# State space stage of a two-block network: a memory tile for each part of a table, two loads into idle buffers, the last inputs scaled behind the first units, and outputs split one step later

## The chip, the cores and the metric

The kernel runs on one core of one Trainium2 chip. The metric is the device time of one execution in microseconds (us), as the median of several runs. A core has five engines that run side by side and meet at semaphores: TensorE (PE, matrix products; its weight loads are listed as PEld), VectorE (DVE), ScalarE (ACT), GpSimd (POOL) and SyncE (SP). Each works through its own instructions in order. SP and ACT also start DMA transfers here, so a transfer that has to wait for a buffer holds up what stands behind it on that engine.

## What is computed

Two blocks on 512 tokens of width 1024 in float32. The first block has two layers; its second layer (index 1) holds the state space mixer that the change is about. Cut to what matters:

```python
h = rms_norm(x, norm_mix[1])
# s5_mixer(h): 64 groups of 16 channels, 64 complex states each
mag = jnp.exp(lr * dt)
ab_re, ab_im = mag * jnp.cos(li * dt), mag * jnp.sin(li * dt)
...
bu_re = jnp.einsum('gpc,bsgc->bsgp', bb_re, uf)
bu_im = jnp.einsum('gpc,bsgc->bsgp', bb_im, uf)
_, _, xr, xi = lax.associative_scan(_complex_affine_combine, (a_r, a_i, bu_re, bu_im), axis=1)
y = (jnp.einsum('gcp,bsgp->bsgc', c_re, xr) - jnp.einsum('gcp,bsgp->bsgc', c_im, xi)
     + d.reshape(S5_GROUPS, S5_GROUP_CH) * uf)
# behind it
g_a, g_b = jnp.split(jax.nn.gelu(y) @ od_w_glu, 2, axis=-1)
x = x + g_a * jax.nn.sigmoid(g_b)
```

Ahead of it lie the first layer's mixer, its convolutional feed-forward network (`conv_ffn`) and a gated side input (`ple`); behind it the second layer's feed-forward network and side input, and the whole second block.

## The kernel before

All activations lie in SBUF with channels on the 128 partitions and the 512 tokens along the free axis, as eight tiles x[0] to x[7]. A matrix product splits each operand into a rounded high part and a low rest (`split`: a cast on ACT, line 308, then a subtraction on DVE, line 311) and adds three products (`mm_fm`, lines 373 to 375). Weights come through SP into `raw` tiles, are cast to `whi` on ACT (line 345) and subtracted to `wlo` on DVE or POOL (line 350).

**Tables.** The mixer works on sequences of four tokens at a time. While `conv_ffn(0)` runs, `s5_tables` makes coefficient tables in sixteen rounds of two quarter tiles and writes them to DRAM (line 1150, on ACT's queue): G (256 columns, makes the scans' input from u), E (256 columns, the rotation's cosine and sine) and C (416 columns, makes the output from u, xr and xi). `CUT` names the columns; `tabs[k]` holds unit k's tables.

**Units.** A unit is one of the eight tiles of 128 channels. `ready(m)` runs as `ple` finishes x[m]: it adds the squares of x[m] to the sum for the norm (`Rms.add`, lines 217 to 225), and `turn_in` scales x[m], writes it to DRAM and reads it back in another order as `up` (four DMAs on SP, line 1247). For m = 1, 3 and 5 it also starts table loads, and for m = 7 it runs a square root on a tile of one column, `warm` (line 1324). When all eight are in, `chain` and `phases` make `rbt`, the factor 1/rms in the order of `up` (lines 174 to 182 and 1339 to 1346; line 177 is the square root on ACT).

A unit then goes through these steps:

- `norm`: up times rbt (line 1250; unit 0 on DVE, the others on POOL)
- `feed`: 16 products on PE, G with up, into two PSUM banks pv (line 1256), and a copy `rm` of the decay (ACT, line 1259)
- `spin`: six DVE instructions that rotate pv by E (lines 1265 to 1270)
- `scan`: two scans along the tokens on DVE (line 1277), giving zr and zi, and products with E that rotate back into xr and xi (lines 1283 to 1295): on POOL for units 0 to 6, on DVE for unit 7; of odd units the difference that gives xr is made by DVE (`real`, line 1295)
- `emit`: products on PE, C with up, xr and xi (line 1303), a gelu on ACT (line 1305), a write to DRAM (line 1306) and a read in the order of the tokens into `y` (four DMAs on SP, line 1310)
- `land`: the split of y into G.h[k] and G.l[k] (lines 308 and 311), the operands of the product with `od_w_glu`.

**Order.** A loop over t runs the units as a pipeline, one step apart: in step t it calls feed(t+1), a load of G for t+3, spin(t), on even t real(t-1), a load of E for t+1 (from t = 2), emit(t-2), a load of C for t, scan(t), land(t-3), and the products of output t-4 with the first weights (`acc0[1]`). At t = 8 the second accumulator `acc0[0]` starts. Table tiles have two buffers for G and C and three for E, y has two. The seven norms of units 1 to 7 stand ahead of the loop. Within these calls the framework's scheduler sets the order on each engine when it builds the program, by order in the code and by when it expects an operand to be ready.

Of the kernel before, what the change touches and what calls it, by code (L numbers as in the profile page):

```python
# [18 lines left out]
P = 128  # L19
# [30 lines left out]
def tile_net(ctx: ExitStack, tc: tile.TileContext, a, out):  # L50
# [5 lines left out]
    def nm(s):  # L56
        uid[0] += 1
        return f"{s}_{uid[0]}"
# [151 lines left out]
    class Rms:  # L210
# [4 lines left out]
        def add(self, m):  # L215
            if self.n == 0:
                act.activation(self.acc, x[m], AF.Square)
            else:
                if self.two and self.n % 2:
                    sq = xp.tile([P, T], F32, tag="diag", name=nm("sq"), bufs=2)  # L220
                else:
                    sq = stile("st_q")
                act.activation(sq, x[m], AF.Square)  # L223
                eng = pool if self.n < 6 else vec
                eng.tensor_tensor(self.acc, self.acc, sq, op=ALU.add)  # L225
            self.n += 1
# [664 lines left out]
    def ple(l, X, rms, done, fins=()):  # L891
        with tc.tile_pool(name=nm("ple"), bufs=1) as pp:
# [73 lines left out]
    r4 = const.tile([P, 32], F32, name="r4")  # L966
    CUT = {"tG": (0, 256), "tE": (704, 960), "tC": (288, 704)}
    tabs = [{z: dr.tile([P, 4, hi - lo], F32, tag=f"{z}{k}", name=f"{z}{k}") for z, (lo, hi) in CUT.items()}
            for k in range(KD)]
    hdr = [dr.tile([P, 4, P], F32, tag=f"hd{k}", name=f"hd{k}") for k in range(KD)]  # L970
# [241 lines left out]
    with tc.tile_pool(name="s5e", bufs=1) as ep, ExitStack() as late:  # L1212
# [6 lines left out]
        class Unit:  # L1219
# [3 lines left out]

            def table(self, tag, bufs):
                lo, hi = CUT[tag]
                t = ep.tile([P, 4, hi - lo], F32, tag=tag, name=nm(tag), bufs=bufs)
                nc.scalar.dma_start(t, tabs[self.k][tag])
                return t

            def load_g(self):  # L1230
                self.G = self.table("tG", 2)

            def load_e(self):
                self.E = self.table("tE", 3)

            def load_c(self):
                self.C = self.table("tC", 2)

# [13 lines left out]
            def feed(self):  # L1252
                self.pv = [bank((P, 4, P)) for _ in range(2)]
                for z in range(2):
                    for i in range(4):
                        pe.matmul(self.pv[z][:, i, :], self.G[:, i, P * z:P * z + P], self.up[:, i, :],
                                  start=True, stop=True)
                self.rm = rms4[self.par]
                act.copy(self.rm[:, :, 1:], r4[:, 4 * self.k:4 * self.k + 4].unsqueeze(2).to_broadcast([P, 4, P - 1]))

            def spin(self):
                pv = self.pv
                er, ei = self.E[:, :, 0:P], self.E[:, :, P:]
                t0, t1 = [xt_(f"X{'hl'[self.par]}{j}") for j in range(2)]
# [7 lines left out]
            def scan(self):  # L1272
# [6 lines left out]
                eng = vec if k == KD - 1 else pool  # L1279
                er, ei = self.E[:, :, 0:P], self.E[:, :, P:]  # L1280
                self.xr, self.xi = xrs[self.par]
# [9 lines left out]
                eng.tensor_tensor(v[1], ei, self.zr, op=ALU.mult)  # L1291
                eng.tensor_tensor(self.xi[:, :, 1:], v[0], v[1], op=ALU.add)

# [3 lines left out]
            def emit(self):  # L1297
                k = self.k
                py = bank((P, 4, P))
                for i in range(4):  # L1300
                    for st, (c, rhs) in enumerate(((288, self.up[:, i, :]), (0, self.xr[:, i, 0:P]),
                                                   (160, self.xi[:, i, 0:P]))):
                        pe.matmul(py[:, i, :], self.C[:, i, c:c + P], rhs, start=st == 0, stop=st == 2)
                g = ep.tile([P, 4, P], F32, tag="h", name=nm("g"), bufs=2)
                act.activation(g, py, AF.Gelu_apprx_tanh)
                nc.scalar.dma_start(hdr[k], g)
                self.y = rp.tile([P, 4, P], F32, tag="y", name=nm("y"), bufs=2)
                src = hdr[k].rearrange("(r c) i n -> i c r n", c=32)
# [11 lines left out]
        def ready(m):  # L1320
            rms2.add(m)
            if m == KD - 1:
                warm = sm.tile([P, 1], F32, tag="warm", name="warm")
                act.activation(warm, eps_r, AF.Sqrt)
            units[m].turn_in()
# [41 lines left out]
        units[0].feed()  # L1367
        units[2].load_g()
        for k in range(1, KD):
            units[k].norm(pool)  # L1370
# [3 lines left out]
        for t in range(KD + 4):  # L1374
# [8 lines left out]
            if t == 2:  # L1383
                acc0[1] = [bank() for _ in range(2)]
            if t > 1 and at(t + 1):
                at(t + 1).load_e()
            if t == KD:
                acc0[0] = [bank() for _ in range(2)]
                mm_fm(acc0[1], w0s[1], G, [4], start=False, stop=False, js=[4])
                for k in range(3):  # L1390
# [5 lines left out]
            if at(t):  # L1396
                at(t).scan()
            if at(t - 3):
                at(t - 3).land()
            if at(t - 4):  # L1400
                k = t - 4
                if t != KD:
                    mm_fm(acc0[1], w0s[1], G, [k], start=k == 0, stop=k == KD - 1, js=[k])
                if t == KD + 1:
# [13 lines left out]
        for c in range(4):  # L1418
# [5 lines left out]
            for j in range(2):  # L1424
                m = 2 * c + j
                sg = rp.tile([P, T], F32, tag="y", name=nm("sg"), bufs=2)
                act.activation(sg, acc0[1][j], AF.Sigmoid)
# [508 lines left out]
```

## Time and profile before

| | us |
|---|---|
| runs: median (lowest to highest of 3) | 2743.25 (2742.7 to 2746.15) |
| the profiled execution | 2745.55 |
| its span, first to last instruction | 2743.8 |
| PE busy | 2692.1 |
| DVE busy | 1562.4 |
| ACT busy | 999.5 |
| POOL busy | 684.0 |

The profile is one execution, seen by the hardware profiler. The span is what the instructions take from first to last; the execution's own time is a little longer. An engine's busy time counts its computing instructions only; waits, branches and the starting of DMAs are not in it. A row of the timeline gives the start in us from the span's beginning, the duration, the engine, the line in the kernel, the operation, what is written and read, the count of instructions merged into the row, and in brackets how long the engine was idle before and what ended that. Names stand without their numbers, so `s` is one of several scratch tiles and `ps` any PSUM bank.

### The profile page before, as it was taken

The page shows a single profiled execution, that of the slowest core. Times are in us where ns is not written, and L with a number is a line of the kernel's source. Part 1 is how long each engine was busy: PE and PEld are TensorE (multiplying, and loading weights), DVE is VectorE, ACT ScalarE, POOL GpSimd, SP SyncE. Part 2 cuts the span into 40 slices and gives each one's busy share as a digit, 9 for nine tenths or more (in the row PEclk, how much of TensorE's full clock was granted, in tenths as well). Part 3 has the DMA queues.
Part 4 walks back from the last instruction along what each step waited for, and adds up shares of the span by engine and source line. Part 5 has one row for each costly group of instructions (what it writes and reads, how often), then busy time and mean ns, then how long its engine had stood idle before and what let it go on. Part 6 is the DMA issues. An engine that isn't in the chain of part 4 may idle for free. (4 is left out here: it accounts for less than half of the span.)

```text
span 2743.8 us, 35312 instructions
## 1 busy us (share of the span) xinstructions
PE 2692.1 (98%) x14355; PEld 2270.6 (83%) x14355; DVE 1562.4 (57%) x2475; ACT 999.5 (36%) x1302; POOL 684.0 (25%) x721
## 2 busy tenths in 40 slices
PE   8999999999799999999999999999999999999998
PEld 8978887887678888888888888888888888888888
DVE  5455989475774746475333335866387755633335
ACT  5543424345433424244212235333343353422222
POOL 2214035553541000002000036454554321200000
PEclk9999999999999999999999999999999999999999
DMA  5214334335652222223322222232322223222231
GB/s 165 73 36 108 100 120 162 122 117 198 223 185 90 96 95 92 93 92 123 107 93 92 92 93 91 89 102 79 98 83 83 92 93 108 78 92 92 93 102 68
DMA packets 278995, 288.79 MB, mean 105 GB/s; under 512 B 20325, under 2 KB 267079, under 8 KB 278832
## 3 DMA queue, kind: packets, MB, share of 16 engines
q1 hardware_dynamic: 243152, 244.65, 27.3%
q10 hardware_dynamic: 34848, 41.46, 4.5%
q8 instruction: 113, 1.85, 0.3%
q0 software_dynamic: 832, 0.41, 0.1%
q14 instruction: 50, 0.41, 0.0%
HBM read 262.90 MB, written 23.59 MB: 104 GB/s over the span
## 5 line engine op out<-in xcount | busy, mean ns | idle before, releaser
L345 ACT CAST whi<-raw 128x2048 fp32r<-128x2048 f32 (+2 forms) x216 | 406.5, 1882 | 777.9 <-PE ps L374 589.5
L373 PE MATMUL ps<-Xh,whi 128*128 128x512 f32 (+1 forms) x1472 | 568.9, 388 | 1.0 <-ACT Xh L308 1.0
L374 PE MATMUL ps<-Xl,whi 128*128 128x512 f32 (+1 forms) x1472 | 564.7, 384 | 1.5 <-DVE Xl L311 1.0
L375 PE MATMUL ps<-Xh,wlo 128*128 128x512 f32 (+1 forms) x1472 | 564.1, 384 | 0.0
L350 DVE TENSOR_TENSOR wlo<-raw,whi 128x2048 fp32r<-128x2048 f32 (+2 forms) x167 | 380.4, 2278 | 318.0 <-ACT whi L345 316.5
L350 POOL TENSOR_TENSOR wlo<-raw,whi 128x512 fp32r<-128x512 f32 (+1 forms) x196 | 248.4, 1299 | 664.8 <-ACT whi L345 340.1
L373 PEld LDWEIGHTS ps<-Xh,whi 128*128 128x128 f32 x1472 | 277.5, 189 | 60.0 <-issue 3.0
L374 PEld LDWEIGHTS ps<-Xl,whi 128*128 128x128 f32 x1472 | 278.7, 189 | 58.2 <-DVE Xl L311 1.4
L375 PEld LDWEIGHTS ps<-Xh,wlo 128*128 128x128 f32 x1472 | 278.1, 189 | 57.0 <-DVE wlo L350 0.4
L373 PE MATMUL ps<-XBh,whi 128*128 128x512 f32 (+1 forms) x736 | 281.9, 385 | 1.0 <-ACT whi L345 1.0
L374 PE MATMUL ps<-XBl,whi 128*128 128x512 f32 (+1 forms) x736 | 281.1, 383 | 0.6 <-POOL XBl L311 0.6
L375 PE MATMUL ps<-XBh,wlo 128*128 128x512 f32 (+1 forms) x736 | 281.6, 384 | 0.0
L375 PE MATMUL ps<-Ah,wlo 128*128 128x512 f32 (+1 forms) x528 | 202.5, 384 | 0.0
L373 PE MATMUL ps<-Ah,whi 128*128 128x512 f32 (+1 forms) x528 | 202.5, 386 | 0.0
L374 PE MATMUL ps<-Al,whi 128*128 128x512 f32 (+1 forms) x528 | 202.1, 383 | 0.3 <-DVE Al L311 0.3
L1604 DVE SCALAR_TENSOR_TENSOR ps<-glu,par,ps 128x512 f32<-128x512 f32 x232 | 170.4, 752 | 3.9
L374 PEld LDWEIGHTS ps<-XBl,whi 128*128 128x128 f32 x736 | 138.2, 188 | 30.6 <-POOL XBl L311 1.0
L375 PEld LDWEIGHTS ps<-XBh,wlo 128*128 128x128 f32 x736 | 138.2, 188 | 29.9
L373 PEld LDWEIGHTS ps<-XBh,whi 128*128 128x128 f32 x736 | 137.7, 188 | 29.5 <-ACT whi L345 1.4
L225 POOL TENSOR_TENSOR st_a<-st_a,st_q 128x512 f32<-128x512 f32 x22 | 38.4, 1747 | 455.1 <-ACT st_q L223 455.0
L382 PE MATMUL ps<-whi,Xh 128*128 128x256 f32 (+1 forms) x512 | 147.4, 289 | 0.5 <-ACT z L616 0.4
L383 PE MATMUL ps<-wlo,Xh 128*128 128x256 f32 (+1 forms) x512 | 144.7, 283 | 0.0
(498 smaller groups left out, 4790.0 us busy)
## 6 DMA issues: line engine op xcount, KB each, us to landing
raw<-in_ffn_w_up_dram SPq DMA_DIRECT2D x66, 1024.0 KB, 5.1
raw<-in_w_in_dram SPq DMA_DIRECT2D x40, 1024.0 KB, 5.1
raw<-in_ffn_w_down_dram SPq DMA_DIRECT2D x32, 1024.0 KB, 4.8
raw<-in_ffn_w_gate_dram SPq DMA_DIRECT2D x22, 1024.0 KB, 5.2
raw<-in_ffn_w_down_dram SPq DMA_DIRECT2D x16, 768.0 KB, 4.2
raw<-in_ev_w_in_dram SPq DMA_DIRECT2D x8, 1024.0 KB, 5.2
raw<-in_ple_w_gate_dram SPq DMA_DIRECT2D x8, 1024.0 KB, 5.1
raw<-in_od_w_glu_dram SPq DMA_DIRECT2D x8, 1024.0 KB, 5.8
```

What stands on the lines that cost most here:

```text
L225: eng.tensor_tensor(self.acc, self.acc, sq, op=ALU.add)
L345: cp = act.copy(hi, rv)
L350: lo.tensor_tensor(lw[:, o:o + q], rv[:, o:o + q], hi[:, o:o + q].bitcast(F32), op=ALU.subtract)
L373: pe.matmul(acc, wh[j][:, s], X.h[k], start=start and t == 0, stop=False)
L374: pe.matmul(acc, wh[j][:, s], X.l[k], start=False, stop=False)
L375: pe.matmul(acc, wl[j][:, s], X.h[k], start=False, stop=stop and t == len(ks) - 1)
L382: pe.matmul(acc, X.h[k][:, s], wh[j], start=start and t == 0, stop=False)
L383: pe.matmul(acc, X.h[k][:, s], wl[j], start=False, stop=False)
L1604: vec.scalar_tensor_tensor(x[m] if t == 30 else acc, u[:, t:t + T], col("ck", t * KD + m), acc, op0=ALU.mult, op1=ALU.add)
```

## The change

- `CUT` names seven parts of 128 columns where it named three: tG and tG2, tE and tE2, tC, tC2 and tC3. Each has a tile of its own in DRAM and in SBUF and a DMA of its own, both when the tables are written (line 1150 of the kernel before) and when they are loaded. Of C the 32 columns that no product reads are left out (416 become 3 x 128).
- `load_g` and `load_e` can be given idle buffers: unit 2's G is loaded into Xh6 and Xl6 and unit 3's E into Xh7 and Xl7, both ahead of the loop. Loads of E in the loop start at t = 3.
- Units 1 to 4 are normed ahead of the loop. The norms of units 5, 6 and 7 are issued in steps 0, 1 and 2, held behind the last POOL instruction of that step's scan (`issue_after`).
- `land` comes at t-4 in place of t-3, y has three buffers, and the products of output 4 with the first weights are in their regular place at t = 8.
- `warm` reads the last square that was added to the norm's sum, and not the constant `eps_r`.

```diff
@@ Rms.add @@
                 act.activation(sq, x[m], AF.Square)
+                self.sq = sq
@@
-    CUT = {"tG": (0, 256), "tE": (704, 960), "tC": (288, 704)}
-    tabs = [{z: dr.tile([P, 4, hi - lo], F32, tag=f"{z}{k}", name=f"{z}{k}") for z, (lo, hi) in CUT.items()}
-            for k in range(KD)]
+    CUT = {"tG": (0, 128), "tG2": (128, 256), "tE": (704, 832), "tE2": (832, 960),
+           "tC": (576, 704), "tC2": (288, 416), "tC3": (448, 576)}
+    tabs = [{z: dr.tile([P, 4, P], F32, tag=f"{z}{k}", name=f"{z}{k}") for z in CUT} for k in range(KD)]
@@ class Unit @@
-            def table(self, tag, bufs):
-                lo, hi = CUT[tag]
-                t = ep.tile([P, 4, hi - lo], F32, tag=tag, name=nm(tag), bufs=bufs)
-                nc.scalar.dma_start(t, tabs[self.k][tag])
-                return t
...
+            def table(self, names, spare):
+                o = []
+                for j, z in enumerate(names):
+                    if spare:
+                        t = xp.tile([P, 4, P], F32, tag=spare[j], name=nm(z))
+                    else:
+                        t = ep.tile([P, 4, P], F32, tag=z, name=nm(z), bufs=3 if z[1] == "E" else 2)
+                    nc.scalar.dma_start(t, tabs[self.k][z])
+                    o.append(t)
+                return o
+
+            def load_g(self, spare=None):
+                self.G = self.table(("tG", "tG2"), spare)
...
@@ ready @@
-                act.activation(warm, eps_r, AF.Sqrt)
+                act.activation(warm, rms2.sq[:, 0:1], AF.Sqrt)
@@ ahead of the loop @@
-        units[2].load_g()
-        for k in range(1, KD):
+        units[2].load_g(("Xh6", "Xl6"))
+        units[3].load_e(("Xh7", "Xl7"))
+        for k in range(1, 5):
             units[k].norm(pool)
@@ the loop @@
-            if t > 1 and at(t + 1):
+            if t > 2 and at(t + 1):
                 at(t + 1).load_e()
             if t == KD:
                 acc0[0] = [bank() for _ in range(2)]
-                mm_fm(acc0[1], w0s[1], G, [4], start=False, stop=False, js=[4])
...
             if at(t):
-                at(t).scan()
-            if at(t - 3):
-                at(t - 3).land()
+                last = at(t).scan()
+                if at(t + 5):
+                    with tc.issue_after(last.ins):
+                        at(t + 5).norm(pool)
+            if at(t - 4):
+                at(t - 4).land()
             if at(t - 4):
                 k = t - 4
-                if t != KD:
-                    mm_fm(acc0[1], w0s[1], G, [k], start=k == 0, stop=k == KD - 1, js=[k])
+                mm_fm(acc0[1], w0s[1], G, [k], start=k == 0, stop=k == KD - 1, js=[k])
```

`scan` now returns its last instruction (the sum that gives xi), and `emit`, `feed` and `spin` take the parts of a table as tiles and not as columns of one.

More of the change, by code (lines that the diff above doesn't have):

```diff
@@ L1222, in __init__, with load_e, load_c @@
                 self.par = k % 2
-            def table(self, tag, bufs):
-                lo, hi = CUT[tag]
-                t = ep.tile([P, 4, hi - lo], F32, tag=tag, name=nm(tag), bufs=bufs)
-                nc.scalar.dma_start(t, tabs[self.k][tag])
-                return t
[L1230 to L1237, printed above, removed]
+            def table(self, names, spare):
[10 more added lines that the diff above has]
+                self.G = self.table(("tG", "tG2"), spare)
+            def load_e(self, spare=None):
+                self.E = self.table(("tE", "tE2"), spare)
+            def load_c(self, spare=None):
+                self.C = self.table(("tC", "tC2", "tC3"), spare)
             def turn_in(self):
@@ L1255, in feed @@
                     for i in range(4):
-                        pe.matmul(self.pv[z][:, i, :], self.G[:, i, P * z:P * z + P], self.up[:, i, :],
+                        pe.matmul(self.pv[z][:, i, :], self.G[z][:, i, :], self.up[:, i, :],
                                   start=True, stop=True)
@@ L1262, in spin @@
                 pv = self.pv
-                er, ei = self.E[:, :, 0:P], self.E[:, :, P:]
+                er, ei = self.E
                 t0, t1 = [xt_(f"X{'hl'[self.par]}{j}") for j in range(2)]
@@ L1279, in scan @@
                 eng = vec if k == KD - 1 else pool
-                er, ei = self.E[:, :, 0:P], self.E[:, :, P:]
+                er, ei = self.E
                 self.xr, self.xi = xrs[self.par]
@@ L1291, in scan @@
                 eng.tensor_tensor(v[1], ei, self.zr, op=ALU.mult)
-                eng.tensor_tensor(self.xi[:, :, 1:], v[0], v[1], op=ALU.add)
+                return eng.tensor_tensor(self.xi[:, :, 1:], v[0], v[1], op=ALU.add)
             def real(self, eng):
@@ L1300, in emit @@
                 for i in range(4):
-                    for st, (c, rhs) in enumerate(((288, self.up[:, i, :]), (0, self.xr[:, i, 0:P]),
-                                                   (160, self.xi[:, i, 0:P]))):
-                        pe.matmul(py[:, i, :], self.C[:, i, c:c + P], rhs, start=st == 0, stop=st == 2)
+                    for st, rhs in enumerate((self.up[:, i, :], self.xr[:, i, 0:P], self.xi[:, i, 0:P])):
+                        pe.matmul(py[:, i, :], self.C[st][:, i, :], rhs, start=st == 0, stop=st == 2)
                 g = ep.tile([P, 4, P], F32, tag="h", name=nm("g"), bufs=2)
@@ L1306, in emit @@
                 nc.scalar.dma_start(hdr[k], g)
-                self.y = rp.tile([P, 4, P], F32, tag="y", name=nm("y"), bufs=2)
+                self.y = rp.tile([P, 4, P], F32, tag="y", name=nm("y"), bufs=3)
                 src = hdr[k].rearrange("(r c) i n -> i c r n", c=32)
@@ L1425, in tile_net @@
                 m = 2 * c + j
-                sg = rp.tile([P, T], F32, tag="y", name=nm("sg"), bufs=2)
+                sg = rp.tile([P, T], F32, tag="y", name=nm("sg"), bufs=3)
                 act.activation(sg, acc0[1][j], AF.Sigmoid)
```

## The prediction

> **What bounds the kernel now.** I read the page first, then busy time by stretch, then the timeline of one stage engine by engine, then its waits.
>
> ```profile
> PE 2692.1 (98%) x14355; PEld 2270.6 (83%) x14355; DVE 1562.4 (57%) x2475; ACT 999.5 (36%) x1302; POOL 684.0 (25%) x721
> ...
> 420.00:470.00 50.00, 50.00 (x298) 40.30 (x299) 48.04 (x94) 23.47 (x36) 39.04 (x64) 0.97 0.50 173
> ...
> 716.00:806.00 90.00, 70.60 (x429) 61.63 (x428) 68.12 (x93) 21.67 (x35) 61.73 (x50) 0.92 0.66 215
> 806.00:900.00 94.00, 94.00 (x410) 75.98 (x409) 44.91 (x42) 34.04 (x37) 11.07 (x5) 1.00 0.28 90
> ```
>
> The first row is the page's: TensorE (PE) is busy for 98% of the span, so only its pauses can be won. The others are busy times by stretch (length, then PE, PEld, DVE, ACT, POOL, each with its instructions, then the granted clock and the DMA share). The state space stage, 716 to 806 us, is the one of these in which PE pauses: 70.6 us busy in 90, so 19.4 us lost, and a granted clock of 0.92. In the stretch in which the tables are made (420 to 470) and behind the stage PE is full. So the change can win some of these 19 us, and nothing else.
>
> What sets the pace inside the stage? First its start, which hangs on one reciprocal root:
>
> ```profile
> L1324 ACT ACTIVATE warm<-eps_r x1: 202/202/202, 2.0 to 2.0; 128x1 f32<-128x1 f32 x1
> ...
> 713.27 0.64 ACT L223 ACTIVATE sq<-x 128x512 f32<-128x512 f32 x1
> ...
> 715.78 0.17 DVE L174 TENSOR_SCALAR ps<-ps 128x4 f32<-128x4 f32 x1 [1.15 <-PE ps L204]
> ...
> 715.89 1.08 ACT L916 COPY Xl<-ps 128x512 f32<-128x512 f32 x2 [0.88 <-PE ps L204]
> ...
> 717.38 1.28 ACT L177 ACT_TABLE_LOAD   x1 [0.41 <-ACT Xl L916]
> 718.67 0.16 ACT L177 ACTIVATE ps<-ps 128x4 f32<-128x4 f32 x1
> ...
> 719.22 0.60 ACT L916 COPY st_s<-ps 128x512 f32<-128x512 f32 x1
> ...
> 720.04 0.30 PEld L1345 LDWEIGHTS ps<-rr,l 128*128 128x128 f32 x2 [1.83 <-ACT st_s L916]
> ...
> 720.57 0.29 DVE L1346 COPY rbt<-ps 128x128 f32<-128x128 f32 x1 [0.60 <-PE ps L1345]
> ```
>
> The warm-up root reads a constant and so runs 2.0 us after the program's start, where it loads no table for this stage. The real root has its input at 715.95 (715.78 + 0.17), but ACT comes to it at 717.38 and loads a table for 1.28 us; rbt, the factor that every norm needs, is there at 720.86.
>
> Then GpSimd (POOL) and VectorE (DVE):
>
> ```profile
> 720.94 11.26 POOL L1250 TENSOR_TENSOR up<-up,rbt 128x512 f32<-128x512 f32 x7 [1.98 <-DMA up<-hd]
> ...
> 726.37 5.84 POOL L1250 TENSOR_TENSOR up<-up,rbt 128x512 f32<-128x512 f32 x3
> ...
> 732.17 1.26 POOL L1284 TENSOR_TENSOR s<-tE,zi 128x512 f32<-128x512 f32 x1
> ...
> 756.02 1.27 POOL L1283 TENSOR_TENSOR s<-tE,zr 128x512 f32<-128x512 f32 x1
> ...
> 758.61 1.62 POOL L1292 TENSOR_TENSOR xi<-s,s 128x512 f32<-128x512 f32 x1
> ...
> 785.75 1.30 POOL L1292 TENSOR_TENSOR xi<-s,s 128x512 f32<-128x512 f32 x1
> ...
> POOL s L1283 <- DVE zr L1277: 3.6, 2, 1.9
> POOL s L1284 <- DVE zi L1277: 0.7, 1, 0.7
> ```
>
> POOL works without a pause from 720.94 to 760.23 (758.61 + 1.62): seven norms, then units 0 to 3. Behind that it waits for a scan three times (the last two rows, from the view of waits: 3.6 us in two, 0.7 in one), and it ends at 787.05. So POOL's part lasts 66.11 us with 4.3 idle. DVE is the other half:
>
> ```profile
> 722.86 0.69 DVE L1265 TENSOR_TENSOR s<-tE,ps 128x512 f32<-128x512 f32 x1 [1.27 <-PE ps L1256]
> ...
> 726.45 1.21 DVE L1277 TENSOR_TENSOR_SCAN zi<-s,ps 128x512 f32<-128x512 f32 x1
> ...
> 727.58 2.26 DVE L350 TENSOR_TENSOR wlo<-raw,whi 128x2048 fp32r<-128x2048 f32 x1
> 729.76 1.21 DVE L1277 TENSOR_TENSOR_SCAN zr<-s,ps 128x512 f32<-128x512 f32 x1
> ...
> 743.26 1.74 DVE L1295 TENSOR_TENSOR xr<-s,s 128x512 f32<-128x512 f32 x1 [2.90 <-POOL s L1283]
> ...
> 754.16 0.69 DVE L1265 TENSOR_TENSOR s<-tE,ps 128x512 f32<-128x512 f32 x1 [1.11 <-DMA tE<-tE]
> ...
> 757.84 1.24 DVE L311 TENSOR_TENSOR Gl<-y,Gh 128x512 fp32r<-128x512 f32 x1 [1.19 <-ACT Gh L308]
> ...
> 760.20 0.68 DVE L1295 TENSOR_TENSOR xr<-s,s 128x512 f32<-128x512 f32 x1
> ...
> 767.16 1.68 DVE L311 TENSOR_TENSOR Gl<-y,Gh 128x512 fp32r<-128x512 f32 x1 [1.06 <-ACT Gh L308]
> ...
> 775.11 1.03 DVE L311 TENSOR_TENSOR Gl<-y,Gh 128x512 fp32r<-128x512 f32 x1 [0.46 <-ACT Gh L308]
> ...
> 790.57 0.69 DVE L1292 TENSOR_TENSOR xi<-s,s 128x512 f32<-128x512 f32 x1
> ```
>
> From the first spin (722.86) to the end of unit 7's products (790.57 + 0.69 = 791.26) DVE waits five times: 2.90 for POOL's products of unit 1, 1.11 for unit 4's table E, and 1.19, 1.06 and 0.46 for the ACT half of a split of outputs that were not back from memory. Sum 6.72. Two serial engines, each over 90% busy, pass units to each other. The stage ends thus:
>
> ```profile
> 803.57 0.40 PE L373 MATMUL ps<-Gh,wr 128*128 128x512 f32 x1
> ...
> 805.15 0.62 ACT L308 CAST Gh<-y 128x512 fp32r<-128x512 f32 x1 [8.02 <-DMA y<-hd]
> ```
>
> When the last output is split (805.15), PE is already multiplying the next weights (wr, from 803.57): behind 791 PE has work throughout, so the length of the last unit's trip through memory is covered. What counts is when PE gets its work before that.
>
> **The change part by part.**
>
> *Warm-up root.* It now reads the last square (made 713.27 to 713.91), so its table load comes about 713.9. ACT shifts by 1.28 less its pauses of 0.88 and 0.41 (rows of the ACT timeline at 715.89 and 717.38), and the root can run about 717.4 in place of 718.67: 1.25 us earlier. PE's next instruction also waited for the copy st_s (719.22 + 0.60 = 719.82), which stands behind the root on ACT and moves with it only as far as PE has made its input. Ends 0 and -1.25; I take **-0.9**, nearer to the root's own row.
>
> *Norms 5 to 7 behind scans 0 to 2, on POOL.* No work goes away; it is reordered. Four norms end at 726.37, where the last three start (5.84 us, 2.1 more than three at 1.26, as L350 ran beside them). Unit 0's first scan ends at 727.66 (726.45 + 1.21). So POOL pauses 1.29 us where it used to norm, and the 2.1 beside L350 falls on a product instead. Against now, unit 0 ends 3 x 1.26 - 1.29 = 2.5 us earlier, unit 1 1.2 (a norm less of gain each), unit 2 about as now, and unit 3 1.29 later. That is a gain only if DVE uses it. Queued behind a held norm on POOL are the next unit's products, which wait 1.26 per norm. PE waits for norm 5 only at feed 5, some four steps on, so no feed is late.
>
> *Split one step on, three buffers y.* DVE and ACT no longer wait for y: -1.19, -1.06, -0.46. The third buffer takes a hold off SP: output 3 need not wait for split 1 to end. The ACT queue is in order, and its casts of y waited long; gelu, table loads and rm copies stood behind:
>
> ```profile
> ACT Gh L308 <- DMA y<-hd: 26.6, 6, 8.0
> ```
>
> ```profile
> 724.12 1.90 ACT L345 CAST whi<-raw 128x2048 fp32r<-128x2048 f32 x1 [4.30 <-DMA pjd<-st_s]
> ```
>
> *Tables.* Unit 3's E is fetched before the loop and unit 4's takes the buffer of unit 0 as before, now a step early against POOL's finish: the 1.11 wait goes. Unit 2's G no longer waits for feed 0, so the cast of the first weights behind it on ACT comes up to 2 us sooner, and L350 (2.26) can start in DVE's pause of 1.27 us before 722.86: 0 to -1.3, I take -0.5.
>
> *DVE's sum.* Its first wait shrinks: real(1) needs unit 1's products on POOL, which move by -2 x 1.26 (norms 6 and 7 gone from in front) + 1.29 = -1.23. From there spin 3 and 4 run on without 1.11, 1.19 and the 1.24 of the split at 757.84: DVE is at real(3) at 760.20 - 1.23 - 1.11 - 1.19 - 1.24 = 755.4. But POOL's unit 3 is 1.29 later than now: the last that real(3) needs ended at 757.29 (756.02 + 1.27), and would end at 758.6. So a **new wait of 3.2 us** comes up, and real(3) starts 1.6 earlier than before, not 4.7. Behind it three splits lie before unit 7's products, as before (one fewer, but one moved in), and 1.06 and 0.46 go: 1.6 + 1.06 + 0.46 = **-3.1**. POOL's own sum agrees: its pauses of 4.3 go and one of 1.29 comes, **-3.0**. I take -3.0, ends 0 (the pauses only move) and -4.3 (no new pause), and beyond it -7 if the port stretches below vanish too.
>
> *PE.* acc0[1] gets each output one step later, so up to 6 matmuls of output 3 lie behind unit 7 that lay before it. One costs 0.23 us (94.00 us for 410 in the stretch behind 806): 0 to +1.4, I take +0.5.
>
> *More DMA instructions on ACT.*
>
> ```profile
> L1150 ACTq DMA_DIRECT2D tG<-tabs x16: 366/366/367, 413.1 to 641.6; - x16
> L1227 ACTq DMA_DIRECT2D tC<-tC x8: 326/430/1212, 656.3 to 781.6; - x8
> ...
> DMA to landing us min/median/max: 1.8/3.9/8.1
> ...
> hd<-h ACTq DMA_DIRECT2D x8, 256.0 KB, 2.7
> ```
>
> While the tables are made, 7 writes stand where 3 stood: 16 x 4 x 0.366 = 23.4 us of ACT's time over some 230 us (first and last start in the row). PE is full there (50.00 of 50 in the row above) and ACT 47% busy (23.47 of 50), so I cost it at nothing; if the cover failed in one place it would be 4 x 0.366 = 1.5. In the stage 7 loads stand where 3 stood: 4 x 0.33 to 0.43 = 1.3 to 1.7 us a unit on an engine that is busy 21.67 of 90 us. Bytes fall, as C is 3 x 128 columns and not 416. I take 0 for the path; the rival below has the other end.
>
> The Trainium skill (SBUF — State Buffer, "The DMA setup-cost knee") speaks against this part: it gives each transfer a fixed time of roughly 2 us and advises to coalesce. Taken one after the other, its four more transfers a unit would be about 8 us a unit (an estimate from that page); the sum by the trace is 0. The last two rows above are the times to landing of y (64 KB each) and of hd (256 KB): 3.9 us for the small and 2.7 for the large, so here landing follows what else moves more than the size.
>
> **Sum:** -0.9 - 3.0 - 0.5 + 0.5 = **-3.9 us**. It is made against the profiled execution, which took 2745.55 us (span 2743.8 and 1.75 around it), 2.3 above the median 2743.25 but inside the runs shown. Taken off the median: 2743.25 - 3.9 = **2739.3**.
>
> **The rivals.**
>
> *A. The waits only move* (chance 0.15). POOL is full to 760.23 and the same work lies before that, so unit 3 may set everything behind it; then only the root is won, -0.9 or less, 2742.4 to 2743.3. For it: unit 3 comes out later in my own sum. Against: the three waits for scans behind 760.
>
> *B. More than the pauses goes* (0.2). A POOL instruction took 1.62 beside DVE (758.61) and 1.26 alone, DVE's splits 1.03 to 1.68 against 0.68 for the same shape at 760.20; if the new order lets them miss each other, and L350 lies in the pause at the start, some 3 more go: about -7, 2736.2. PE has 19.4 to give. Against: the engines are as full as before, and so will meet as often.
>
> *C. ACT becomes the bound* (0.08), slower. Its queue is in order, and a table load whose buffer is not free holds up the gelu and the cast behind it. If the 1.7 us of more issues lie on the path of units 3 to 7, and a held buffer once per unit is not hidden, it is 5 x 1.7 = 8.5, less 0.9: +7.6, 2750.9. It decides once ACT's work and issues for a unit (21.67 / 8 + 7 x 0.33 = 5.0 us) plus its holds exceed POOL's 7.8 us a unit ((787.05 - 732.17) / 7). For it: an issue of a load of table C took up to 1.21 us. Against: ACT's long waits were for y, which are taken away.
>
> *D. The transfers stand one behind the other* (0.02). By the row of y a 64 KB transfer landed in no less than 1.8 us; four more in series are 7.2 us a unit, and units 4 to 7 have all their loads in the loop: +29, 2772. The Trainium skill, SBUF — State Buffer, "The DMA setup-cost knee", would have it so. Against: 256 KB landed in 2.7 us, not four times 1.8.
>
> **How the numbers follow.** Forecast 0.55, with its own range -6.9 to -1.6, 2736.4 to 2741.7 (-1.25 - 4.3 - 1.3 + 0 at one end; 0 - 3.0 + 0 + 1.4 at the other). The change doing nothing it says is in A. A measurement of this kernel tells 0.2%, about 5.5 us, from no change. Faster by that: a fifth of the forecast's 0.55 and nearly all of B, 0.11 + 0.19 = 0.30. Slower: most of C, and D, 0.08. Same: 0.62. The range takes in the forecast, A and most of B, and leaves out C, D and B's far end: 2734 to 2746.
>
> **What would show it.** Right: a table load at about 714 and none before the root; rbt by 720.3; no wait of the cast Gh for y over 2 us; POOL at unit 0 before 729, then a DVE wait of about 3 us before real(3); unit 7's products end by 788. Wrong: POOL ends unit 6 at 787 as before (A); ACT table loads with waits ahead of a gelu (C); PE pauses behind 790, which would mean that work for PE now comes too late for its cover.

## The result, and the profile after

| | before | changed |
|---|---|---|
| median (lowest to highest), us | 2743.4 (2742.7 to 2746.15), 4 runs | 2756.86 (2753.7 to 2758.37), 4 runs |
| the profiled execution | 2745.55 | 2753.7 |
| its span | 2743.8 | 2751.9 |

The changed kernel is slower: ratio 1.005, 95% interval 1.0038 to 1.0063, or 13.5 us between the medians. Forecast were 2739.3 and a range up to 2746. The profiled execution of the changed kernel was the shortest of its four, so its trace holds only 8.1 us of the 13.5 (2751.9 - 2743.8). Those 8.1 can be placed by four marks that both traces have: the last square of the norm, the copy into rbt, the last product of unit 7, and the end.

| stretch | before | changed | difference |
|---|---|---|---|
| start to last square | 713.27 | 718.98 | +5.7 |
| last square to rbt | 7.30 | 9.39 | +2.1 |
| rbt to unit 7's last product | 70.00 | 68.97 | -1.0 |
| from there to the end | 1953.2 | 1954.6 | +1.3 |

So the largest loss lies ahead of the stage that the prediction was about. Busy time by stretch (length, then PE, PEld, DVE, ACT, POOL, then the granted clock, the DMA share and GB/s): the first part of the making of the tables, before and changed, and then from rbt to unit 7's last product, before and changed:

```profile
365.00:470.00 105.00, 101.23 (x575) 81.77 (x574) 97.21 (x187) 37.13 (x51) 61.02 (x98) 0.97 0.46 156
365.00:470.00 105.00, 97.01 (x554) 77.08 (x553) 90.81 (x174) 34.52 (x46) 54.93 (x92) 0.98 0.47 142
...
720.57:790.57 70.00, 52.67 (x340) 47.19 (x341) 61.87 (x79) 13.27 (x20) 61.53 (x46) 0.90 0.68 226
728.37:797.34 68.97, 51.03 (x308) 46.37 (x308) 61.36 (x79) 12.72 (x18) 59.79 (x46) 0.81 0.69 217
```

From 365 to 470 PE is busy for 4.2 us less than before. It was not quite full there before either: it lacked 3.77 of the 105, in one pause that ended at 418. From rbt to unit 7 PE is busy for 51.03 where it was 52.67, at a clock of 0.81 where it was 0.90.

**The tables.** The view of waits between 365 and 660 us, for PE and then DVE (engine, tile and line, what it waited for: us in total, times, the longest), first before, then changed:

```profile
PE ps L1137 <- DVE cv L864: 3.8, 1, 3.8
...
DVE x L883 <- PE ps L375: 21.6, 6, 6.1
...
DVE tabs L1146 <- ACT tabs L1144: 10.3, 10, 7.1
```

```profile
PE ps L1138 <- DVE cv L865: 5.0, 2, 3.3
...
PE ps L376 <- DVE wlo L351: 1.6, 1, 1.6
...
DVE tabs L1147 <- ACT tabs L1145: 41.1, 14, 6.4
...
DVE x L884 <- PE ps L376: 1.6, 1, 1.6
```

The lines of the changed kernel are up to ten further on (L865 is L864 of before, L1145 is L1144). Before, DVE's additions into x stood 21.6 us waiting for PE: DVE was ahead of PE. Now they stand 1.6, DVE waits 41.1 us for ACT's copies into the tables where it was 10.3, and all of PE's waits in this view come to 9.9 us where they were 5.1. The first of the new ones, from the timelines (start, duration, engine, line, operation, what is written and read, in brackets the idle time before and what ended it; ACTq is a DMA issue in ACT's queue), first before, then changed:

```profile
367.79 1.91 ACT L345 CAST whi<-raw 128x2048 fp32r<-128x2048 f32 x1 [9.29 <-PE ps L374]
...
381.73 0.39 PE L373 MATMUL ps<-Xh,whi 128*128 128x512 f32 x1
```

```profile
363.80 0.90 ACTq L1151 DMA_DIRECT2D tE<-tabs  x2
...
372.24 1.12 POOL L1176 TENSOR_TENSOR tabs<-tb 64x160 f32<-64x160 f32 x2
...
373.38 2.55 ACTq L1151 DMA_DIRECT2D tC<-tabs  x2
...
377.64 1.90 ACT L346 CAST whi<-raw 128x2048 fp32r<-128x2048 f32 x1 [19.08 <-issue]
...
381.92 0.50 PE L376 MATMUL ps<-Xh,wlo 128*128 128x512 f32 x1 [1.59 <-DVE wlo L351]
...
385.85 0.45 PE L374 MATMUL ps<-Xh,whi 128*128 128x512 f32 x1
```

Both casts are of the same weights. Before, the cast comes behind two writes of table E, at 367.79. In the changed kernel ACT's order has seven writes ahead of it (two of E, two of C and three of E), and it comes at 377.64. Issuing the seven takes about 3 us; the rest is standing. From 364.7 (363.80 + 0.90) ACT stands with the first part of C until POOL has made its columns, at 373.36 (372.24 + 1.12). Whole, as it was before, C was first written at 418.5, so nothing of it stood here.

Before, the cast was done at 369.70, 9.3 us ahead of the first product that reads it (378.98). Now PE waits 0.40 us for the cast and 1.59 for DVE's subtraction behind it, and then runs at about half speed until 385.85. The two last PE rows are the thirteenth product with these weights, before and changed: it is 4.1 us late, of the 5.7. PE's longest pause there in the changed kernel, 3.3 us until 421.76, is not new: before, PE paused 3.77 us ahead of the same products, until 418.02.

**The root.** The timeline of the changed kernel between the last square and rbt:

```profile
718.98 0.64 ACT L223 ACTIVATE sq<-x 128x512 f32<-128x512 f32 x1
...
719.64 1.28 ACT L1329 ACT_TABLE_LOAD   x1
...
724.05 2.07 ACTq L922 DMA_DIRECT2D pjd<-Xl  x2
...
726.16 0.16 ACT L177 ACTIVATE ps<-ps 128x4 f32<-128x4 f32 x1 [1.97 <-DMA up<-hd]
...
728.37 0.29 DVE L1351 COPY rbt<-ps 128x128 f32<-128x128 f32 x1 [0.90 <-PE ps L1350]
```

The table load does come right behind the last square, and none stands ahead of the root. But ACT is idle for 1.97 us before the root at 726.16, and the end of that is the landing of a transfer, which the root doesn't read: the two issues of pjd<-Xl ahead of it in ACT's order took 2.07 us, until 726.12 (before, the same two took 0.84).

**The units.** POOL and DVE in the changed kernel's timeline, and then, from its view of waits, those of the cast Gh:

```profile
735.07 2.29 DVE L351 TENSOR_TENSOR wlo<-raw,whi 128x2048 fp32r<-128x2048 f32 x1
...
739.17 1.26 POOL L1290 TENSOR_TENSOR s<-tE,zi 128x512 f32<-128x512 f32 x1 [4.95 <-DVE zi L1283]
...
767.93 1.73 DVE L1301 TENSOR_TENSOR xr<-s,s 128x512 f32<-128x512 f32 x1 [3.04 <-POOL s L1289]
...
797.34 0.68 DVE L1298 TENSOR_TENSOR xi<-s,s 128x512 f32<-128x512 f32 x1
```

```profile
ACT Gh L309 <- DMA y<-hd: 17.3, 5, 5.3
```

POOL's pause ahead of unit 0's products is 4.95 us. DVE's subtraction of the weights (735.07) stands ahead of the first scan, where before it stood behind it (727.58). The new DVE wait ahead of the difference xr of unit 3 is there, 3.04 us.

### The profile page after: what moved, and what is told of

It is laid out like the page before. It is cut to its first block, busy times and chain, and to the rows that moved or that the text cites. A ratio compares the mean times of both kernels' runs of the same rounds, so it can differ in the third digit from the quotient of the medians.

```text
span 2751.9 us, 35494 instructions
## 1 busy us (share of the span) xinstructions
PE 2693.7 (98%) x14355; PEld 2270.7 (83%) x14355; DVE 1560.9 (57%) x2475; ACT 1001.5 (36%) x1303; POOL 677.7 (25%) x721
```

## The experiments

Lines of code are cut to the core. A number in brackets behind a difference of two medians is its 95% interval, from drawing the runs of both again. Every median stands beside runs of the kernel before on the same chip.

| run | median us (runs) | before | ratio, 95% interval |
|---|---|---|---|
| e1 | 2747.01 (11) | 2743.39 | 1.0014 (1.0006 to 1.0023) |
| e2 | 2749.14 (11) | 2743.39 | 1.0019 (1.0010 to 1.0028) |
| e3 | 2752.31 (6) | 2743.39 | 1.0031 (1.0020 to 1.0043) |
| e4 | 2744.23 (11) | 2743.39 | 1.0001 (0.9992 to 1.0010) |
| e5 | 2746.78 (12) | 2743.31 | 1.0011 (1.0003 to 1.0020) |
| e6 | 2742.89 (12) | 2743.31 | 0.9994 (0.9985 to 1.0004) |
| e7 | 2745.04 (12) | 2743.31 | 1.0006 (0.9998 to 1.0014) |
| e8 | 2741.53 (12) | 2743.31 | 0.9992 (0.9983 to 1.0001) |
| e9 | 2857.65 (4) | 2742.93 | 1.0425 (1.0408 to 1.0443) |
| e10 | 2739.85 (11) | 2742.93 | 0.9984 (0.9975 to 0.9993) |
| e11 | 2741.68 (11) | 2742.93 | 0.9996 (0.9987 to 1.0005) |
| e12 | 2751.32 (7) | 2743.47 | 1.0029 (1.0018 to 1.0040) |

### e1 to e4: one part alone, or one part undone

**e1** is the kernel before with tables in seven parts, written and loaded one by one, and nothing else of the change.

```diff
-    CUT = {"tG": (0, 256), "tE": (704, 960), "tC": (288, 704)}
+    CUT = {"tG": (0, 128), "tG2": (128, 256), "tE": (704, 832), "tE2": (832, 960),
+           "tC": (576, 704), "tC2": (288, 416), "tC3": (448, 576)}
```

> The kernel before, with the tables in seven parts of 128 columns (seven writes a round, seven loads a unit) and nothing else of the change. Theory W (the writes while the tables are made cost the time): the last square of the stage, at 713.3 us in the kernel before and 719.0 in the changed one, comes at 717 to 720, and the run is 4 to 10 us slower than the kernel before. Rival R (the later order of norms and splits costs it): the last square stays within 1 us of 713.3, and the run is within 3 us of the kernel before.

Its last square comes at 719.3, as late as in the changed kernel (718.98), though nothing else was changed, and the largest waits of PE between 365 and 660 are nearly the changed kernel's:

```profile
PE ps L1137 <- DVE cv L864: 5.2, 2, 3.8
...
PE ps L375 <- DVE wlo L350: 1.6, 1, 1.6
```

Its median is 3.6 us above that of before. The part alone delays the square, and the cast of the weights comes at 377.15, behind the same seven writes. The 3.6 is just under the 4 to 10 expected.

**e2** is the changed kernel with three writes a round, into the three DRAM tensors of before; the loads still come in parts, by column slices.

```diff
+    CUT = {"tG": (0, 256), "tE": (704, 960), "tC": (288, 704)}
...
-                    nc.scalar.dma_start(t, tabs[self.k][z])
+                    nc.scalar.dma_start(t, part(self.k, z))
```

> The changed kernel, but the tables are written with three DMAs a round into DRAM tensors of 256, 256 and 416 columns, as before; the loads stay in parts (column slices, rows of 512 bytes). Theory W: the last square is back at 713.3 within 1 us, and the run is 4 to 9 us faster than the changed kernel, so 4 to 10 us slower than the kernel before. Rival R: no more than 2 us faster than the changed kernel. If rows of 512 bytes make the loads late, DVE or PE waits for tC, tE or tG grow by more than 3 us in sum, and the gain is smaller.

The last square is back at 712.9, and 7.7 us of the 13.5 (4.6 to 9.4) are gone. The cast is back too, at 367.74. e1 and e2 together show that the loss is in the writes and not in the loads of parts, which e2 keeps. Why the writes cost 7.7 in the changed kernel and 3.6 alone, the runs don't say.

**e3** is the changed kernel with the warm root on the constant again, **e4** the kernel before with the warm root on the last square.

```diff
-                act.activation(warm, rms2.sq[:, 0:1], AF.Sqrt)
+                act.activation(warm, eps_r, AF.Sqrt)
```

> The changed kernel with the warm-up root on the constant again. Theory H (the table load ahead of the last input's scaling holds up ACT's queue of copies and writes): from the last square to rbt it takes 7.0 to 7.5 us, as before the change (7.3), and not 9.4 as in the changed kernel, and the run is 1 to 4 us faster than the changed kernel. Rival P (as predicted): without it the root waits for its table, and the run is about 1 us slower than the changed kernel.

> The kernel before with the warm-up root on the last square and nothing else of the change. Theory H: from the last square to rbt 8.5 to 9.5 us in place of 7.3, and 1 to 3 us slower than the kernel before. Rival P (as predicted): 6.0 to 6.7 us, and 0.6 to 1.2 us faster.

From the last square to rbt it is 7.4 us in e3, 9.4 in e4, 7.3 and 9.4 in the kernels before and changed. Undone, the part gives back 4.5 us (1.4 to 6.1), a little more than the 1 to 4 expected; alone it costs 0.8, less than the 1 to 3 expected and not told from nothing by its interval, though the same hold is in its trace:

```profile
721.38 0.16 ACT L177 ACTIVATE ps<-ps 128x4 f32<-128x4 f32 x1 [2.35 <-DMA pjd<-Xl]
```

The root has stood 2.35 us when it runs, until a write landed. So the warm root wins nothing and delays rbt in both; what it costs in the median differs between the two bases.

### e5 to e8: the rest, step by step

**e5** is e2 and e3 together (three writes, root on the constant). **e6** is e5 with the split at its old step and the products of output 4 in their old place; **e7** is e5 with all seven norms ahead of the loop; **e8** has the edits of e6 and e7 both, so that what is left of the change is loads in parts, the idle buffers and a third y. The two edits:

```diff
-            if at(t - 4):
-                at(t - 4).land()
+            if at(t - 3):
+                at(t - 3).land()
```

```diff
-        for k in range(1, 5):
+        for k in range(1, KD):
             units[k].norm(pool)
...
-                last = at(t).scan()
-                if at(t + 5):
-                    with tc.issue_after(last.ins):
-                        at(t + 5).norm(pool)
+                at(t).scan()
```

> The changed kernel with three writes a round (as in e2) and the warm-up root on the constant (as in e3): what is left of the change are loads in parts, the idle buffers, norms behind scans, splits one step on and three buffers y. Theory W + H + L (writes, root, and a third loss behind the units because the splits come a step later): the last square at 713.3 and rbt 7.3 later, both within 1 us, and still 2 to 6 us slower than the kernel before, with the time from unit 7's last product to the end 3 to 5 us longer than in the kernel with parts alone (1948.0 in e1). Rival W + H (those two are the whole loss): within 2 us of the kernel before.

> As e5, with the splits at step t-3 and the order of the products of output 4 as before. Theory L: 3 to 5 us faster than e5, and the time from unit 7's last product to the end is back near 1948 to 1950; PE's waits for Gh and Gl inside the units' loop shrink. Rival (the later split is harmless): within 1.5 us of e5.

> As e5, with all norms ahead of the loop. If the norms behind the scans win 1 us or more, as the prediction had it (its POOL sum: pauses of 4.3 us against one of 1.3): rbt to unit 7's last product is 1 to 3 us longer than in e5, and the run as much slower. Rival A of the prediction (POOL's work is only reordered): within 1 us of e5.

> As e5, with both undone: norms ahead, splits at step t-3. Left are loads in parts, the idle buffers and three buffers y. Theory: rbt to unit 7's last product 68 to 69 us against 70.0 in the kernel before, as in e1, nothing lost elsewhere, so 0.5 to 2.5 us faster than the kernel before. Rival: the shorter wait for tables is not on the path, within 0.5 us.

The later split costs 3.9 us (2.6 to 8.0) between e5 and e6, 3.5 (2.9 to 5.6) between e7 and e8. The norms behind scans cost 1.7 (0.2 to 2.8) between e5 and e7, and 1.4 between e6 and e8, where the interval (-2.5 to 3.1) holds nothing too. e8 is 1.8 us below the kernel before, an interval that just reaches it. Of what was expected, the time from unit 7's last product to the end is 1955.9 us in e5, 7.9 more than in e1 and so beyond the 3 to 5, and back at 1948.8 in e6. From rbt to unit 7 it is 66.7 us in e7 against 68.8 in e5: shorter, where a win by the norms would have made it 1 to 3 longer; and the median is 1.7 lower, more than the rival's 1. In e8 it is 68.4, as expected.

Where the split's loss lies, by stretches cut at rbt, unit 7's last product and the first sigmoid, in e7 (late split) and e8 (old step), length first, then PE busy with its count, and the clock third from the end:

```profile
718.60:785.30 66.70, 49.39 (x306) 44.97 (x307) 61.39 (x79) 12.79 (x18) 61.83 (x46) 0.80 0.81 218
785.30:805.50 20.20, 19.61 (x110) 16.48 (x109) 5.89 (x10) 6.97 (x12) 0.00 (x0) 1.00 0.52 146
```

```profile
720.60:789.00 68.40, 55.02 (x348) 49.58 (x348) 61.55 (x81) 13.84 (x20) 62.01 (x46) 0.88 0.82 225
789.00:804.70 15.70, 15.70 (x79) 13.06 (x78) 5.16 (x9) 5.83 (x10) 0.00 (x0) 1.00 0.44 134
```

With the later split the units are through sooner (66.7 us in place of 68.4), but PE did 306 instructions beside them and not 348, at a clock of 0.80 and not 0.88, and 110 and not 79 are left behind the last unit. PE pays 4.5 us there (20.2 - 15.7) for 1.7 won. By the view of lines for the first row of each, 28 of the 42 products that PE had not done are products that make outputs (144 in e7, 172 in e8), and 14 are products of outputs with weights (34 and 48); and in e7 PE stood 5.6 us in this stretch for the cast Gh, in e8 not at all. So in e7 PE stands for a late output with other work behind it in its order.

Where the norms lose, by POOL's waits from rbt to unit 7, e5 first, then e7:

```profile
POOL s L1294 <- DVE zi L1287: 4.7, 1, 4.7
```

```profile
POOL s L1294 <- DVE zi L1287: 0.6, 1, 0.6
```

With the norms held back, POOL stands 4.7 us for the scan of the first unit, with nothing to do that it could have normed.

### e9 and e12: number of writes, or size of rows?

In the changed kernel the writes are both more and smaller. **e9** is e8 and four more writes a round on ACT's queue of one column each into tensors that nothing reads; **e12** the same with one row of 512 B each.

```diff
+                for o in {"tG": (128,), "tE": (832,), "tC": (288, 448)}[z]:
+                    d = dr.tile([P, 1], F32, tag=f"dm{it}_{o}", name=nm("dm"))
+                    nc.scalar.dma_start(d, tab[:, 0, o:o + 1])
```

```diff
+                    d = dr.tile([1, 1, P], F32, tag=f"dm{it}_{o}", name=nm("dm"))
+                    nc.scalar.dma_start(d, tab[0:1, 0:1, o:o + P])
```

> Against e8_parts_and_buffers (three writes a round): four more writes a round on ACT's queue, each of one column (128 rows of 4 B), so that the count a round is seven as in the changed kernel while the table's own rows keep their size. Theory (it is the number of writes in ACT's queue, and the order of the stage that it brings): unit 7's last square 5 to 6 us later than e8's 710.3, at 715 to 717 or beyond, and the median 4 to 8 us above e8's 1.0-kernel median of 2741.5, ratio to before 1.0010 to 1.0022. Rival (it is the size of the rows, 512 B and less in place of more): last square within 1.5 us of e8's, ratio 0.9985 to 1.0000.

> Against e8_parts_and_buffers (three writes a round): four more writes a round on ACT's queue, each of one single row of 512 B, so that the count is seven a round while the bytes and rows of the tables stay as they were. It replaces e9, whose 4-byte rows took some 12.9 us each to land and filled the queues themselves. Theory (it is the number of writes between ACT's instructions, and the order of ACT and DVE that goes with it): unit 7's last square 4 to 8 us later than e8's 710.3, PE waits for DVE's cv or POOL's tabs of some 5 us or more in 365 to 660, the median 4 to 9 us above e8's (ratio to before 1.0007 to 1.0024). Rival (the loss is of the rows cut to 512 B and their packets): last square within 1.5 us of e8's and the ratio 0.9983 to 1.0000.

e9 can't tell the two apart: it is 116 us slower than e8, far beyond both expectations, and its transfers are slow themselves; the view of DMA issues between 365 and 710 us (KB each, median us from issue to landing), e9 and then the changed kernel:

```profile
raw<-in_ffn_w_up_dram SPq DMA_DIRECT2D x12, 1024.0 KB, 13.9
...
dm<-tabs ACTq DMA_DIRECT2D x57, 0.5 KB, 12.9
```

```profile
raw<-in_ffn_w_up_dram SPq DMA_DIRECT2D x12, 1024.0 KB, 5.5
```

A write of 512 bytes in 128 rows of 4 B landed after 12.9 us, and the weights loaded beside them after 13.9 where it was 5.5.

e12 leaves the tables' rows as they are. Its 64 extra writes carry 32 KB in all, and it loses 9.8 us against e8 (8.5 to 11.2), a little above the 4 to 9 expected; its last square comes at 722.1, 11.8 later than e8's, of which 2.1 are there already at the cast ahead of the tables (344.60 against 342.55). The rival, the size of the rows, expected 1.5 at most. From e12's timeline, and then its largest wait of PE between 365 and 660:

```profile
372.44 2.45 ACTq L1158 DMA_DIRECT2D dm<-tabs  x2
...
376.67 1.91 ACT L346 CAST whi<-raw 128x2048 fp32r<-128x2048 f32 x1 [18.38 <-POOL tb L1180]
```

```profile
PE ps L376 <- DVE wlo L351: 4.7, 3, 2.1
```

So more writes in ACT's queue are enough to lose these microseconds, with next to no bytes and with the tables' rows left long. But two of e12's four writes a round read columns of C that POOL makes early, and they take the same place as the parts of C in the changed kernel: they stand ahead of the cast, which comes at 376.67 and in e8 at 365.53. So e12 does not tell the number of writes from the place that some of them get. In the programs, e1, e12 and the changed kernel all have ACT's and DVE's instructions of this stage in another order than before, and the kernels with three writes have the order of before; PE's order is the same in e12 as in e8. At the cast, the standing in that order is most of the delay (about 3 us of issuing in 9.9 us); for the losses behind it these runs don't separate the two. A version with seven writes that stand behind the cast, or in another engine's queue, was not run.

### e10 and e11: was ACT held by an issue?

**e10** is e8 with six of the eight writes of the projection (pjd) issued by POOL, which is idle there; **e11** is e10 with the warm root on the last square.

```diff
-                    nc.scalar.dma_start(pjd[m0 + j], o)
+                    (nc.gpsimd if m0 < 6 else nc.scalar).dma_start(pjd[m0 + j], o)
```

> Against e8_parts_and_buffers: six of the eight writes of the projection go on POOL's queue, which is idle at 703 to 720 us, in place of ACT's. Theory (ACT, which issues in order, stood behind a write that waited for an earlier transfer to land): the time from the last square to the copy into rbt falls from e8's 10.3 us to 7.3 or less, the median 1 to 3 us below e8's (ratio to before 0.9980 to 0.9989). Rival (ACT was held by something else, or POOL's later work takes the gain back): the time stays at 9 to 10.5 us or the median within 1 us of e8's.

> e10 and the warm root on the last square as in the changed kernel. Theory (the warm root lost only because ACT stood behind a write): last square to rbt 5.5 to 6.7 us, 0.9 to 1.3 less than e10's, and the median 0.5 to 1.5 us below e10's. Rival (the root's order itself costs): last square to rbt 8.5 us or more, the median 1 to 3 us above e10's.

In e8 the root's table load stood behind a write too, with the warm root on the constant:

```profile
717.18 1.28 ACT L177 ACT_TABLE_LOAD   x1 [3.20 <-DMA pjd<-Xh]
```

e10 and then e11 between the last square and rbt, and the longest wait of PE for an input in e11:

```profile
714.21 0.62 ACT L223 ACTIVATE sq<-x 128x512 f32<-128x512 f32 x1
...
716.93 1.28 ACT L177 ACT_TABLE_LOAD   x1
...
718.22 0.16 ACT L177 ACTIVATE ps<-ps 128x4 f32<-128x4 f32 x1
...
720.12 0.29 DVE L1355 COPY rbt<-ps 128x128 f32<-128x128 f32 x1 [0.60 <-PE ps L1354]
```

```profile
715.23 0.62 ACT L223 ACTIVATE sq<-x 128x512 f32<-128x512 f32 x1
...
715.87 1.28 ACT L1333 ACT_TABLE_LOAD   x1
...
719.34 0.17 ACT L177 ACTIVATE ps<-ps 128x4 f32<-128x4 f32 x1
...
721.25 0.29 DVE L1355 COPY rbt<-ps 128x128 f32<-128x128 f32 x1 [0.60 <-PE ps L1354]
```

```profile
PE ps L1266 <- DMA up<-hd: 3.2, 1, 3.2
```

The hold is gone in both: 5.9 us in e10 and 6.0 in e11, where e8 had 10.3. That it was the issue that held ACT is shown. e10's median is 1.7 below e8's (4.2 to 0.0 below), within what was expected; its last square came 3.9 later than e8's in the profiled execution, and 2.9 of that are there already at the cast at 345.43 (342.55 in e8), ahead of all that the edit touches. e10 is the one version whose interval lies wholly below the kernel before, by a small step: 0.9984 (0.9975 to 0.9993), or 3.1 us.

e11's 6.0 lies in the 5.5 to 6.7 expected, but it is not the 0.9 to 1.3 less than e10's that the theory asked for, and the median is 1.8 us above e10's (0.3 to 4.9). The root runs 4.1 us behind the last square, in e10 4.0: ACT works without a pause from the square to the root in both, so the table load of 1.28 only changes places with work that is needed too. That work is h of the last unit, 2.0 us behind the square's start in place of 0.5 (717.27 in e11, 714.73 in e10); its write and read come later, and PE waits 3.2 us for an input (last row), a wait that e10 does not have. That this wait is the 1.8 us is not shown.

## Why the prediction was wrong

Its sum, -3.9 us, against what the runs gave, part by part along after, e2, e5, e6, e8 and before (medians):

| term of the sum | predicted | measured |
|---|---|---|
| seven writes a round | 0 | +7.7 (after - e2) |
| warm root | -0.9 | +2.4, 0.9 to 3.9 (e2 - e5) |
| PE's later products (split one step on) | +0.5 | +3.9 (e5 - e6) |
| norms behind scans, tables, L350 | -3.0 and -0.5 | +1.4 (e6 - e8) and -1.8 (e8 - before) |
| sum | -3.9 | +13.6 |

The parts were undone in this one order, and the medians come from several chips, on which the kernel before had 2742.9 to 2743.5. Alone, the writes cost 3.6 (e1) and the root 0.8 (e4). The rows don't map one to one either: the 3.0 also holds DVE's waits for y, which the later split was to take away.

- **The writes: the step that failed.** "PE is full there (50.00 of 50 in the row above) and ACT 47% busy (23.47 of 50), so I cost it at nothing". The term was priced by the time that an issue takes, 0.366 us, and left out that a write stands in ACT's order until its table is made, with what is behind it. The cover named was the wrong one too. That PE is full tells that its inputs came early enough, not by how much; ACT's idle share counts no standing; and the row with 50.00 of 50 begins just behind PE's pause of 3.77 us. What covered the cast of the weights was its lead of 9.3 us, and it came 9.9 us later, most of it behind a part of C that stood for POOL: 4.1 us of the 5.7 (the tables, above). The price for a cover gone was 1.5, at one place. DVE's lead went with it (its waits for PE fell from 21.6 us to 1.6); that this alone would have cost PE time is not shown.
- **The warm root: wrong in sign.** "ACT shifts by 1.28 less its pauses of 0.88 and 0.41". The load did move to right behind the square. But ACT's work between square and root was not looked at as a queue of DMA issues, which can stand: they held the root for 1.97 us in the changed kernel. And e11 shows that without the hold there is nothing to win: the load then stands ahead of the last unit's h, and the root is no earlier.
- **Split one step on: mis-sized, and right only in direction.** "Up to 6 matmuls of output 3 lie behind unit 7": it was 31 more instructions (110 against 79), and 4.5 us to the first sigmoid where 0 to 1.4 stood. Not counted was that PE stands for the late output itself (5.6 us for the cast Gh in e7, none in e8), with the products that make later outputs behind it.
- **DVE's and POOL's stage.** The new wait was predicted at 3.2 us and is 3.04. But POOL's pause for the first scan was taken as 1.29 and is 4.95: DVE's subtraction of the weights, 2.29 us, came ahead of that scan, and POOL has no norm left to fill the time. From rbt to unit 7's last product the changed kernel won 1.0 of the 3.0, and that was lost again behind it (+1.3, or some 4.6 by the clock dip told below).
- **Signs that were named.** A table load right behind the square: yes. rbt by 720.3: no, 728.37, of which 5.7 us come from the late square. No wait of the cast Gh for y over 2 us: no, 5.3 was the longest of 17.3 us in all. POOL at unit 0 before 729: no; counted from rbt it came 10.8 us later, where it was 11.6. DVE's wait: yes. Unit 7 by 788: no, 797.34.
- **The rivals.** C, with 0.08, named the right cause in kind, ACT's queue in order, and the right side of no change; but it looked for it in units 3 to 7, and it is in the making of the tables and ahead of the root. A, the waits only move, comes nearest for the norms, which won nothing and cost 1.4 to 1.7. B's further gain and D's chain of transfers are not seen: no run with the change's order of units gained, and e8 loads in parts and is not slower.

What stays open: how the writes' 7.7 us divide between the issues and the other order behind the cast; and the time to the end behind unit 7, where single dips of the granted clock differ from one execution to the next. In the profiled execution of before PE had pauses of 0.98, 0.30 and 0.59 us between 1662 and 1666, and a dip behind them:

```profile
1664.00:1672.00 8.00, 7.23 (x35) 7.01 (x36) 4.24 (x14) 1.42 (x5) 0.86 (x2) 0.59 0.00 0
```

In the changed kernel the same products come 11 us later, with the same three pauses, and the clock from 1675 to 1683 is 1.00. The dip took some 3.3 us of before (0.41 of 8, an estimate). So the loss behind unit 7 is rather 4.6 than the 1.3 of the table.

## What to carry to other kernels

A full engine's cover is the lead of what feeds it, and that lead is read from the time between an operand's end and its first use, not from the busy share of a third engine. A DMA issue is an instruction in the queue of its engine: count it in that order, with what it may stand for, before splitting one transfer into two; put issues on a queue that is idle there. Pipelining a step later empties the engine behind it first and loads it at the end: count what is left behind the last unit.

## What was not expected of the hardware

PE ran at half speed after a pause of 3.8 us. From the timeline of the changed kernel, and then the clock by stretch:

```profile
745.38 0.79 PE L1308 MATMUL ps<-xr,tC 128*128 128x128 f32 x2 [3.84 <-POOL xr L1301]
...
747.62 0.63 PE L1308 MATMUL ps<-xr,tC 128*128 128x128 f32 x2
748.05 0.63 PE L1308 MATMUL ps<-xi,tC 128*128 128x128 f32 x2
```

```profile
382.00:386.00 4.00, 4.00 (x11) 3.14 (x12) 4.00 (x13) 0.00 (x0) 0.00 (x0) 0.57 0.72 225
...
746.00:750.00 4.00, 3.57 (x17) 3.40 (x17) 3.58 (x7) 0.00 (x0) 4.00 (x4) 0.50 0.20 65
```

Behind a pause of 3.84 us pairs of products start 0.43 us apart, until about 751, and the granted clock is 0.50 in the last row; later they start 0.22 apart (755.22 and 755.44). In one such stretch of 5.6 us (745.38 to 751.03) PE loses about half, 2.8 us by this estimate, nearly as much as the pause; that the stage is longer by it is not shown. The Trainium skill (TensorE: Matmul & The Clock Gate, "What's actually happening") states that an idle window of about 3.4 us halves the array's clock and about as long a busy one restores it; the pause of 3.84 agrees, and the recovery here took 5.6. But in the making of the tables pauses of 0.40 and 1.59 us were followed by the clock of 0.57 in the row before the last, so here shorter pauses were enough.

Rows of 4 B were far dearer than their bytes here (e9: 12.9 us to landing for 512 bytes). The Trainium skill (DMA: Bandwidth & Descriptors, "Specifications") asks for at least 512 B for line rate; the runs agree in direction: as many writes of a single row of 512 B each (e12) cost 9.8 us against e8, and these 116.
